# Rotary embedding on one core: the two leading fp32 positions on two hardware DMA queues, with one table on each

## The chip, the cores and the metric

The kernel runs on one core of a Trainium2 chip. The metric is the device time of one execution in microseconds (us). Before the change it was 317.61 us, the median of 3 runs (317.57 to 317.75).

The profile's span, from the first to the last instruction, is about 1.8 us shorter than the time of the same execution (316.0 us against 317.78 us in the profiled run of the kernel before). Spans are compared with spans below, and times with times.

## The reference

```python
# x: (8, 2048, 16, 64) fp32; cos, sin: (2048, 32) fp32
x1, x2 = x_pairs[..., 0], x_pairs[..., 1]        # neighbours in the last axis
out1 = x1 * cos - x2 * sin
out2 = x1 * sin + x2 * cos
out = np.stack([out1, out2], axis=-1)            # interleaved again, fp32
```

There is little arithmetic per byte. The input is 64 MiB and so is the output: 8 batches of 8 MiB each way.

## The kernel before

A partition holds 16 positions (K = 16) of 1024 values. Each batch is loaded by one transfer issued from GpSimd, which casts fp32 to bf16 on the way. VectorE rotates it in place with three bf16 instructions per four positions, and GpSimd issues the store, which casts back. Five batch tiles (NX = 5) are in use.

The first two positions of batch 0 go another way: as fp32 on the SP queue, then a cast on ScalarE (called ACT in the profile). The last four positions of the last batch leave as fp32 on the SP queue.

```python
    with tc.manual_schedule():
        head = stage.tile([P, TAIL, HD], fp32, name="st")
        for k in range(HEAD):                                   # HEAD = 2
            nc.sync.dma_start(out=head[:, k : k + 1], in_=x_t[0, :, k : k + 1])
        nc.sync.dma_start(out=cos_sb, in_=cos_t)
        nc.sync.dma_start(out=sin_sb, in_=sin_t)
        load(0, HEAD)                                           # GpSimd queue
        for b in range(1, NX):
            load(b)

        nc.scalar.copy(out=tiles[0][:, :HEAD], in_=head[:, :HEAD])
        # ... VectorE: s_tab from sin_sb (two instructions), c_tab from cos_sb ...
        for b in range(B):
            # ... rotate(b, ...) on VectorE, four positions at a time ...
            if b < B - 1:
                store(b)                                        # GpSimd queue
            if b >= 1 and b - 1 + NX < B:
                load(b - 1 + NX)                                # waits for store(b - 1)
        store(B - 1, K - TAIL)

        tail = stage.tile([P, TAIL, HD], fp32, name="st")
        nc.scalar.copy(out=tiles[B - 2][:1, 0, :1], in_=tiles[B - 1][:1, K - 1, :1])   # waits for store(B - 2)
        nc.scalar.copy(out=tail, in_=tiles[B - 1][:, K - TAIL :])
        nc.sync.dma_start(out=out_t[B - 1, :, K - TAIL :], in_=tail)
```

Of the kernel before, what the change touches and what calls it, by code (L numbers as in the profile page):

```python
# [2 lines left out]

# [4 lines left out]


@with_exitstack  # L10
def kernel(
    ctx: ExitStack,
    tc: tile.TileContext,
    x: bass.AP,
    cos: bass.AP,
    sin: bass.AP,
    out: bass.AP,
):
    nc = tc.nc
    fp32 = mybir.dt.float32  # L20
    bf16 = mybir.dt.bfloat16
    mult = mybir.AluOpType.mult
    add = mybir.AluOpType.add

    B, S, H, D = x.shape
    P = 128
    K = S // P
    KP = 4
    D2 = D // 2
    HD = H * D  # L30
    NX = 5
    HEAD = 2
    TAIL = 4


    x_t = x.rearrange("b (p k) h d -> b p k (h d)", p=P, k=K)
    out_t = out.rearrange("b (p k) h d -> b p k (h d)", p=P, k=K)
    cos_t = cos.rearrange("(p k) c -> p (k c)", p=P, k=K)
    sin_t = sin.rearrange("(p k) c -> p (k c)", p=P, k=K)

    consts = ctx.enter_context(tc.tile_pool(name="consts", bufs=1))
    xpool = ctx.enter_context(tc.tile_pool(name="xpool", bufs=NX))
    qpool = ctx.enter_context(tc.tile_pool(name="qpool", bufs=1))
    stage = ctx.enter_context(tc.tile_pool(name="stage", bufs=1))

    cos_sb = consts.tile([P, K * D2], fp32)
    sin_sb = consts.tile([P, K * D2], fp32)
    c_tab = consts.tile([P, K, D], bf16)
    s_tab = consts.tile([P, K, D], bf16)

    tiles = {}

    def load(b, k0=0):
        if b not in tiles:
            tiles[b] = xpool.tile([P, K, HD], bf16, name="xt")
        nc.gpsimd.dma_start(out=tiles[b][:, k0:], in_=x_t[b, :, k0:])  # L56

    def store(b, k1=K):
        nc.gpsimd.dma_start(out=out_t[b, :, :k1], in_=tiles[b][:, :k1])  # L59

    def rotate(b, k0, k1):
        nk = k1 - k0
        xp = tiles[b][:, k0:k1]
        qt = qpool.tile([P, KP, HD], bf16, name="qt")

        def rows(a):
            return a.rearrange("p k (h e) -> p k h e", h=H, e=D)

        def tab(a):
            return dataclasses.replace(  # L70
                a, offset=a.offset + k0 * D, ap=[a.ap[0], [D, nk], [0, H], [1, D]]
            )

        nc.vector.tensor_tensor(out=rows(qt[:, :nk]), in0=rows(xp), in1=tab(s_tab), op=mult)  # L74
        nc.vector.tensor_tensor(out=rows(xp), in0=rows(xp), in1=tab(c_tab), op=mult)  # L75
        q_swap = dataclasses.replace(
            qt, offset=qt.offset + 1, ap=[qt.ap[0], [2, nk * HD // 2], [-1, 2]]
        )
        x3 = xp.rearrange("p k (a j) -> p (k a) j", j=2)
        nc.vector.tensor_tensor(out=x3, in0=x3, in1=q_swap, op=add)  # L80

    with tc.manual_schedule():
        head = stage.tile([P, TAIL, HD], fp32, name="st")
        for k in range(HEAD):
            nc.sync.dma_start(out=head[:, k : k + 1], in_=x_t[0, :, k : k + 1])  # L85
        nc.sync.dma_start(out=cos_sb, in_=cos_t)
        nc.sync.dma_start(out=sin_sb, in_=sin_t)
        load(0, HEAD)
        for b in range(1, NX):
            load(b)  # L90

        nc.scalar.copy(out=tiles[0][:, :HEAD], in_=head[:, :HEAD])  # L92
        s2 = s_tab.rearrange("p k (i j) -> p (k i) j", j=2)
        nc.vector.tensor_copy(out=s2[:, :, 0], in_=sin_sb)  # L94
        nc.vector.tensor_scalar_mul(s2[:, :, 1], sin_sb, -1.0)  # L95
        nc.vector.tensor_copy(  # L96
            out=c_tab.rearrange("p k (i j) -> p (k i) j", j=2),
            in_=cos_sb.to_broadcast([P, K * D2, 2]),
        )
        for b in range(B):  # L100
            if b == 0:
                rotate(b, 0, HEAD)
                rotate(b, HEAD, KP)
            for k0 in range(KP if b == 0 else 0, K, KP):
                rotate(b, k0, k0 + KP)
            if b < B - 1:
                store(b)

            if b >= 1 and b - 1 + NX < B:
                load(b - 1 + NX)  # L110
        store(B - 1, K - TAIL)



        tail = stage.tile([P, TAIL, HD], fp32, name="st")
        nc.scalar.copy(out=tiles[B - 2][:1, 0, :1], in_=tiles[B - 1][:1, K - 1, :1])  # L116
        nc.scalar.copy(out=tail, in_=tiles[B - 1][:, K - TAIL :])  # L117
        nc.sync.dma_start(out=out_t[B - 1, :, K - TAIL :], in_=tail)


# [1 line left out]
_INS = ['x', 'cos', 'sin']  # L122
_OUTS = [((8, 2048, 16, 64), 'float32')]


# [23 lines left out]
```

## Time and profile before

| what | kernel before |
|---|---|
| measured time | 317.61 us |
| span of the profile | 316.0 us |
| VectorE busy | 70% |
| VectorE's wait for the sin table | 44.2 us |
| share of the DMA engines' span, GpSimd queue + hardware queue | 96.8% + 3.1% |
| HBM traffic | 67.63 MB read, 67.11 MB written |

The page of the kernel before begins so. Under "busy tenths", each column is a fortieth of the span:

```profile
DVE 221.8 (70%) x102; ACT 6.9 (2%) x4; POOL 8.9 (3%) x20
...
DVE  0000039999999999999999999999999999100000
...
DMA  9899999999999999999999999999999999999996
...
q0 software_dynamic: 2304, 98.04, 96.8%
q1 hardware_dynamic: 720, 3.67, 3.1%
...
HBM read 67.63 MB, written 67.11 MB: 426 GB/s over the span
```

Read the three kinds of line together. The DVE line (VectorE) has a visible hole at the start. The DMA line has none until the last slice. The queue lines say the same in numbers: 96.8% and 3.1% of 16 engines' span are 99.9%.

The view of waits names the hole:

```profile
ACT xt L116 <- DMA out_dram<-xt: 286.3, 1, 286.3
POOL out_dram L59 <- DVE xt L80: 202.1, 8, 70.5
POOL xt L56 <- DMA out_dram<-xt: 51.3, 3, 21.7
DVE s_tab L94 <- DMA sin_sb<-in_sin_dram: 44.2, 1, 44.2
...
```

Each line gives engine and line, what it waited for, us in total, number of waits, and the longest. VectorE waits once, for sin, and never for a batch load. The large waits of ACT and POOL (GpSimd) are waits of engines that have nothing else to do.

Three lines of the timeline: the issue of store 0, VectorE's last instruction, and the tail's cast (start, duration, engine and line, and in brackets the idle time before it and what ended it).

```profile
74.53 0.54 POOL L59 DMA_DIRECT2D out_dram<-xt  x1 [70.48 <-DVE xt L80]
...
267.11 2.29 DVE L80 TENSOR_TENSOR xt<-xt,qt 128x4096 bf16<-128x4096 bf16 x1
...
295.96 3.60 ACT L117 CAST st<-xt 128x4096 f32<-128x4096 bf16 x1
```

The DMA issues on the page say how long each transfer took from issue to landing (the last column, us):

```profile
xt<-in_x_dram POOLq DMA_DIRECT2D x1, 3584.0 KB, 22.7
...
st<-in_x_dram SPq DMA_DIRECT2D x2, 512.0 KB, 4.5
cos_sb<-in_cos_dram SPq DMA_DIRECT2D x1, 256.0 KB, 22.4
sin_sb<-in_sin_dram SPq DMA_DIRECT2D x1, 256.0 KB, 42.1
```

A table of 256 KB takes as long as a batch load of 3584 KB. The trace's DMA packet records explain it. They are summarised here by queue and size, from the kernel before:

```
queue    bytes written   packets   mean us   first start   last start
GpSimd   28672            128       2.130      5.14          21.43      (batch 0, 14 positions)
GpSimd   32768            896       2.437     22.78         235.04      (loads: 64 KB read, 32 KB written)
GpSimd   65536            896       2.447    101.24         292.96      (stores)
SP       2048             256       0.096      7.25          43.59      (the two tables, 8 packets each on every engine)
```

A table packet needs 0.096 us but is followed by a batch-load packet of over 2 us each time. The batch loads begin at 5.14 us, and the first table packet at 7.25 us, so every table packet pays that turn.

### The profile page before, as it was taken

What the parts mean: (1) busy time and instruction counts of PE and PEld (TensorE: products, weight loads), DVE (VectorE), ACT (ScalarE), POOL (GpSimd) and SP (SyncE); (2) the same over time, 40 slices, a digit from 0 to 9 for tenths busy, and PEclk for the clock granted to TensorE, in tenths of its full rate; (3) what the DMA queues carried; (4) which work ended last, traced back from release to release, by engine and by line L of the source; (5) the groups of instructions that cost most, each with busy time, mean ns of one, the idle gap of its engine ahead of it and who ended that gap; (6) DMA issues with size and microseconds to landing.
All of it is one profiled execution on the core that took longest, in us unless ns stands there. A gap on an engine that the chain in (4) does not pass through costs nothing.

```text
span 316.0 us, 198 instructions
## 1 busy us (share of the span) xinstructions
DVE 221.8 (70%) x102; ACT 6.9 (2%) x4; POOL 8.9 (3%) x20
## 2 busy tenths in 40 slices
DVE  0000039999999999999999999999999999100000
ACT  1200000000000000000000000000000000000400
POOL 3000000000000000000000000000000000000000
DMA  9899999999999999999999999999999999999996
GB/s 241 198 257 212 212 207 236 228 199 199 253 212 265 398 498 431 398 332 261 203 399 465 328 203 199 481 448 265 199 307 423 398 440 481 406 398 481 417 431 263
DMA packets 3025, 101.72 MB, mean 322 GB/s; under 512 B 336, under 2 KB 336, under 8 KB 848
## 3 DMA queue, kind: packets, MB, share of 16 engines
q0 software_dynamic: 2304, 98.04, 96.8%
q1 hardware_dynamic: 720, 3.67, 3.1%
q14 instruction: 1, 0.01, 0.0%
HBM read 67.63 MB, written 67.11 MB: 426 GB/s over the span
## 4 chain that ended last, share of the span: by engine, by line
another core or an unknown queue 91%; DMA 2%; ACTq 1%; ACT 1%; SPq 0%; issue 0%
DMA st<-in_x_dram 2%; ACTq L144 1%; ACT xt L92 1%; ACT L92 0%; SPq L85 0%; ACT xt L116 0%; ACTq L116 0%; ACTq L92 0%
## 5 line engine op out<-in xcount | busy, mean ns | idle before, releaser
L75 DVE TENSOR_TENSOR xt<-xt,c_tab 128x4096 bf16<-128x4096 bf16 (+1 forms) x33 | 73.5, 2228 | 1.1
L80 DVE TENSOR_TENSOR xt<-xt,qt 128x4096 bf16<-128x4096 bf16 (+1 forms) x33 | 73.5, 2228 | 1.1
L74 DVE TENSOR_TENSOR qt<-xt,s_tab 128x4096 bf16<-128x4096 bf16 (+1 forms) x33 | 73.5, 2228 | 1.1
L94 DVE CAST s_tab<-sin_sb 128x512 bf16<-128x512 f32 x1 | 0.5, 453 | 44.2 <-DMA sin_sb<-in_sin_dram 44.2
L59 POOL DMA_DIRECT2D out_dram<-xt x8 | 4.3, 535 | 202.1 <-DVE xt L80 202.1
L116 ACT COPY xt<-xt 1x1 bf16<-1x1 bf16 x1 | 0.2, 193 | 286.3 <-DMA out_dram<-xt 286.3
L56 POOL DMA_DIRECT2D xt<-in_x_dram x8 | 4.4, 561 | 52.1 <-DMA out_dram<-xt 51.3
L117 ACT CAST st<-xt 128x4096 f32<-128x4096 bf16 x1 | 3.6, 3599 | 0.0
L92 ACT CAST xt<-st 128x2048 bf16<-128x2048 f32 x1 | 1.9, 1899 | 0.0
L92 ACT ACT_TABLE_LOAD x1 | 1.3, 1283 | 6.4 <-DMA st<-in_x_dram 6.4
L96 DVE CAST c_tab<-cos_sb 128x1024 bf16<-128x1024 f32 x1 | 0.7, 684 | 0.0
L95 DVE TENSOR_SCALAR s_tab<-sin_sb 128x512 bf16<-128x512 f32 x1 | 0.4, 443 | 0.0
L133 POOL MEMSET const-float32-0.0<- 128x1 f32 x1 | 0.1, 99 | 0.2 <-issue 0.2
L133 POOL MEMSET const-bfloat16-1.0<- 128x1 bf16 x1 | 0.1, 102 | 0.0
L133 POOL MEMSET const-float32-1.0<- 128x1 f32 x1 | 0.1, 99 | 0.0
L133 POOL MEMSET const-uint8-127<- 128x1 uint8 x1 | 0.1, 99 | 0.0
## 6 DMA issues: line engine op xcount, KB each, us to landing
xt<-in_x_dram POOLq DMA_DIRECT2D x7, 4096.0 KB, 58.0
out_dram<-xt POOLq DMA_DIRECT2D x1, 6144.0 KB, 49.4
xt<-in_x_dram POOLq DMA_DIRECT2D x1, 3584.0 KB, 22.7
out_dram<-st SPq DMA_DIRECT2D x1, 2048.0 KB, 15.5
st<-in_x_dram SPq DMA_DIRECT2D x2, 512.0 KB, 4.5
cos_sb<-in_cos_dram SPq DMA_DIRECT2D x1, 256.0 KB, 22.4
sin_sb<-in_sin_dram SPq DMA_DIRECT2D x1, 256.0 KB, 42.1
out_dram<-xt POOLq DMA_DIRECT2D x7, 54.0
```

The lines of the kernel that those rows point to most:

```text
L56: nc.gpsimd.dma_start(out=tiles[b][:, k0:], in_=x_t[b, :, k0:])
L59: nc.gpsimd.dma_start(out=out_t[b, :, :k1], in_=tiles[b][:, :k1])
L74: nc.vector.tensor_tensor(out=rows(qt[:, :nk]), in0=rows(xp), in1=tab(s_tab), op=mult)
L75: nc.vector.tensor_tensor(out=rows(xp), in0=rows(xp), in1=tab(c_tab), op=mult)
L80: nc.vector.tensor_tensor(out=x3, in0=x3, in1=q_swap, op=add)
L92: nc.scalar.copy(out=tiles[0][:, :HEAD], in_=head[:, :HEAD])
L94: nc.vector.tensor_copy(out=s2[:, :, 0], in_=sin_sb)
L95: nc.vector.tensor_scalar_mul(s2[:, :, 1], sin_sb, -1.0)
L96: nc.vector.tensor_copy(out=c_tab.rearrange("p k (i j) -> p (k i) j", j=2), in_=cos_sb.to_broadcast([P, K * D2, 2]),)
L117: nc.scalar.copy(out=tail, in_=tiles[B - 1][:, K - TAIL :])
L133: nc = _bacc.Bacc("TRN2", target_bir_lowering=False, num_devices=1)
L144: with _tile.TileContext(nc) as tc:
```

## The change

The intent is to bring the head (the two fp32 positions) and the tables in sooner by using both hardware queues: each carries one head position and then one table.

```diff
         for k in range(HEAD):
-            nc.sync.dma_start(out=head[:, k : k + 1], in_=x_t[0, :, k : k + 1])
+            q = (nc.sync, nc.scalar)[k % 2]
+            q.dma_start(out=head[:, k : k + 1], in_=x_t[0, :, k : k + 1])
         nc.sync.dma_start(out=cos_sb, in_=cos_t)
-        nc.sync.dma_start(out=sin_sb, in_=sin_t)
+        nc.scalar.dma_start(out=sin_sb, in_=sin_t)
```

## The prediction

> **What bounds the kernel now.** The DMA engines, from end to end. The page's queue table gives the GpSimd queue 96.8% and the hardware queue 3.1% of the 16 engines' span. HBM traffic is 67.63 + 67.11 MB: 426 GB/s over 316 us. The trace's packet records show why this does not move: a batch load reads 64 KB per packet in 2.437 us and a store writes 64 KB in 2.447 us, so 16 engines do about 430 GB/s either way. The GpSimd queue's packets run from 5.14 to 311.76 us; per engine their durations add to about 305.3 us, so that queue is never empty. VectorE is busy 70% and idle for 44.2 us at the start, a wait for the sin table (view of waits). That is the most visible hole, but not what the span waits for.
>
> **Why the tables are late.** Each table is 8 packets of 2 KB per engine, 0.096 us each, and each takes its turn with a 64 KB-read packet of the batch loads: 8 x (2.437 + 0.096) = 20.3 us per table. On one queue cos lands at 24.1 us and sin at 44.2 us. The Trainium skill (DMA: Bandwidth & Descriptors, "Queues, rings and completion order") says an engine goes round its queues packet by packet; this trace agrees, 20.1 us between the landings.
>
> **What the change does.** No byte, packet or compute instruction is added. One head position and sin go from the SP to the Activation queue (two issues of about 0.4 us each move). The tables now take turns beside each other, so both land at about 24 us. VectorE starts at 24-25 us instead of 44.2 and runs 20 us ahead. Batch 0's remaining load landed at 23.9 us, so it is no obstacle.
>
> **How much is on the critical path.** Nearly nothing. The GpSimd queue is served in order: loads 0-4 until 102 us, then store 0, store 1, load 5, store 2, load 6 and so on. Store 0 will be issued at about 54 instead of 74.5 us but still starts at 102. Load 5 waits for store 0 to land (121.5 us) as before. The 20 us come back as VectorE waits: load 6 landed at 199.1 us, VectorE would want it at 194 (about 5 us); load 7 landed at 237.8 against 227 (about 11 us). VectorE ends at about 266 instead of 269.4 us. Store 6 still lands at about 296 us; the tail's cast (3.6 us) waits for that, then comes the 15.5 us tail store. The skill (same page, "Issuing engines are not separate DMA queues") says that another issuing engine saves only issue time.
>
> What can move is the first 5 us, before the GpSimd queue starts: table packets may pass before 5.14 us. Estimate: all 16 per engine would save 16 x 0.096 = 1.5 us, a few 0.2-0.4 us.
>
> **Predicted:** 317.3 us, 8 in 10 within 316.3 to 318.1. Faster by over 2%: 2%; within 2%: 97%; slower: 1%.
>
> **What would show it.** Right: VectorE's wait for a table falls from 44.2 to about 24 us; cos and sin both land about 22 us after issue; new VectorE waits on batch loads of about 16 us in all near 194-238 us; the GpSimd queue's share stays near 97%; the tail's cast still starts near 296 us. Wrong: sin still at 44 us, or VectorE without new waits.
>
> **What would make it wrong.** GpSimd-queue packets other than 2.44 us with three queues active; a start of that queue other than 5.1 us; descriptor writing on GpSimd slowed by VectorE being busy from 24 us; a fixed cost of a second hardware queue.

## The result, and the profile after

The changed kernel takes 317.64 us (median of 6 runs, 317.57 to 317.95) against 317.60 us for the kernel before (median of 6, 317.56 to 317.75). The ratio is 1.0002, 95% interval 0.9989 to 1.0015: the same.

The page after:

```profile
DVE 221.8 (70%) x102; ACT 6.9 (2%) x4; POOL 8.8 (3%) x20
...
DVE  0009999999999999999999994799708996000000
...
DMA  9999999999999999999999999999999999999997
...
q0 software_dynamic: 2304, 98.04, 97.0%
q1 hardware_dynamic: 432, 2.88, 2.4%
q10 hardware_dynamic: 288, 0.79, 0.6%
...
HBM read 67.63 MB, written 67.11 MB: 427 GB/s over the span
```

The hole in the DVE line is half as long at the start, and new holes have opened about two thirds of the way through. The DMA line is as full as it was. The new queue q10 is the Activation queue.

The waits after:

```profile
ACT xt L117 <- DMA out_dram<-xt: 286.8, 1, 286.8
POOL out_dram L59 <- DVE xt L80: 153.9, 5, 50.0
POOL xt L56 <- DMA out_dram<-xt: 95.6, 3, 39.7
DVE s_tab L95 <- DMA sin_sb<-in_sin_dram: 23.8, 1, 23.8
DVE qt L74 <- DMA xt<-in_x_dram: 16.7, 2, 10.8
```

VectorE's wait for sin fell by 20.4 us (44.2 to 23.8). Two waits for batch loads, 16.7 us together, are new. The rest of the 20.4 us is idle time after its last instruction: VectorE began its last add at 263.26 us instead of 267.11, 3.85 us sooner. 16.7 + 3.85 is 20.5 us. GpSimd shows the same thing from the other side: it waits 48.2 us less for VectorE (202.1 to 153.9) and 44.3 us more for stores to land (51.3 to 95.6).

In the timeline after, the two new waits look like this:

```profile
23.77 0.45 DVE L95 CAST s_tab<-sin_sb 128x512 bf16<-128x512 f32 x1 [23.77 <-DMA sin_sb<-in_sin_dram]
...
54.07 0.54 POOL L59 DMA_DIRECT2D out_dram<-xt  x1 [50.03 <-DVE xt L80]
...
199.03 2.29 DVE L74 TENSOR_TENSOR qt<-xt,s_tab 128x4096 bf16<-128x4096 bf16 x1 [5.92 <-DMA xt<-in_x_dram]
...
237.67 2.29 DVE L74 TENSOR_TENSOR qt<-xt,s_tab 128x4096 bf16<-128x4096 bf16 x1 [10.76 <-DMA xt<-in_x_dram]
...
263.26 2.29 DVE L80 TENSOR_TENSOR xt<-xt,qt 128x4096 bf16<-128x4096 bf16 x1
...
295.78 3.60 ACT L118 CAST st<-xt 128x4096 f32<-128x4096 bf16 x1
```

Store 0 is issued at 54.07 us instead of 74.53. It joins a queue that still has 48 us of loads in it. The tail's cast starts at 295.78 us (295.96 before).

The landings of the GpSimd queue's transfers, read from the trace, show where nothing moved (us from the start of the span):

```
          load 1   load 3   load 4   store 0   load 5   load 6   load 7   store 6
before    44.03    82.62   102.18    121.51   160.89   199.13   237.78   295.77
after     43.31    81.96   102.35    121.70   160.29   198.93   237.57   295.58
```

Loads 1 to 3 land 0.7 us sooner, because more packets of the hardware queues now pass before the batch loads start. Behind that start there were 256 table packets and 27 head packets before, 1.80 us of packet time per engine; after, there are 203 and 1, 1.16 us. By load 4 that lead is gone. Experiments e10 and e11 look at this.

### The profile page after: what moved, and what is told of

Its sections match the earlier page's. It is cut to its first block, busy times and chain, and to the rows that moved or that the text cites. A ratio compares the mean times of both kernels' runs of the same rounds, so it can differ in the third digit from the quotient of the medians.

```text
span 315.8 us, 198 instructions
## 1 busy us (share of the span) xinstructions
DVE 221.8 (70%) x102; ACT 6.9 (2%) x4; POOL 8.8 (3%) x20
## 4 chain that ended last, share of the span: by engine, by line
another core or an unknown queue 91%; DMA 2%; ACTq 1%; ACT 1%; issue 0%
DMA st<-in_x_dram 2%; ACTq L145 1%; ACT xt L93 1%; ACT L93 0%; ACT xt L117 0%; ACTq L117 0%; ACTq L93 0%
## 5 line engine op out<-in xcount | busy, mean ns | idle before, releaser
L74 DVE TENSOR_TENSOR qt<-xt,s_tab 128x4096 bf16<-128x4096 bf16 (+1 forms) x33 | 73.5, 2228 | 17.7 <-DMA xt<-in_x_dram 16.7
L95 DVE CAST s_tab<-sin_sb 128x512 bf16<-128x512 f32 x1 | 0.5, 454 | 23.8 <-DMA sin_sb<-in_sin_dram 23.8
L59 POOL DMA_DIRECT2D out_dram<-xt x8 | 4.3, 533 | 153.9 <-DVE xt L80 153.9
L56 POOL DMA_DIRECT2D xt<-in_x_dram x8 | 4.4, 560 | 96.4 <-DMA out_dram<-xt 95.6
```

The lines of the kernel that those rows point to most:

```text
L56: nc.gpsimd.dma_start(out=tiles[b][:, k0:], in_=x_t[b, :, k0:])
L59: nc.gpsimd.dma_start(out=out_t[b, :, :k1], in_=tiles[b][:, :k1])
L74: nc.vector.tensor_tensor(out=rows(qt[:, :nk]), in0=rows(xp), in1=tab(s_tab), op=mult)
L95: nc.vector.tensor_copy(out=s2[:, :, 0], in_=sin_sb)
```

## The experiments

The theory ("DMA-bound"): the GpSimd queue never runs dry, so the time is the start of that queue plus its bytes plus the tail, and VectorE has slack. The rivals: (a) VectorE's chain does set the span; (b) the earlier VectorE start is worth something, and a third queue costs as much again, so that the two cancel.

### e1 and e2: each part of the change alone

e1, against the kernel before:

```diff
-        nc.sync.dma_start(out=sin_sb, in_=sin_t)
+        nc.scalar.dma_start(out=sin_sb, in_=sin_t)
```

> Part alone: only the sin table moves to the Activation queue, both head positions stay on SP. DMA-bound theory: sin gets a turn of its own, so it and cos take their turns beside each other and VectorE's wait for a table ends near 24 us, as in the full change; time 317.3 to 317.9 us all the same. Rival 'the earlier VectorE start does save time and a third queue eats it': also a third queue, so no difference in time, but load packets longer than 2.437 us. Rival 'VectorE-bound': faster than before by several us.

e2, against the changed kernel:

```diff
-        nc.scalar.dma_start(out=sin_sb, in_=sin_t)
+        nc.sync.dma_start(out=sin_sb, in_=sin_t)
```

> Part alone: only the second head position moves to the Activation queue, both tables stay on SP one behind the other. DMA-bound theory: cos lands near 20 us as after (some of its packets pass before the batch loads start), sin follows it and lands near 40 us; VectorE starts near 40 us; time 317.3 to 317.9 us. So the 20 us of VectorE start come from the sin move, and neither part moves the time.

Measured: e1 317.49 us, ratio to before 1.0001 (0.9986 to 1.0016). e2 317.78 us, ratio 1.0011 (0.9994 to 1.0027). Both times are as expected. The VectorE waits of e1 were not as I expected:

```profile
DVE c_tab L96 <- DMA cos_sb<-in_cos_dram: 25.2, 1, 25.2
...
DVE qt L74 <- DMA xt<-in_x_dram: 9.2, 1, 9.2
DVE s_tab L94 <- DMA sin_sb<-in_sin_dram: 5.8, 1, 5.8
```

In e1 sin has its queue to itself and lands at 5.8 us, ahead of the batch loads. Cos lands at 31.8 us, not 24, because the second head position is in front of it on the SP queue and took until 13.2 us. In e2 sin landed at 35.7 us (expected near 40).

So my attribution in e2's text, that all 20 us come from the sin move, was wrong. VectorE has its last table 12.4 us sooner through the sin move alone (44.2 to 31.8) and 8.5 us sooner through the head move alone (44.2 to 35.7). Together the change gives 20.4. Each part takes packets off the SP queue, and it is the number of packets in front that counts. Neither part moves the time. The load packets of e1 last 2.437 us as before, but that is no test of rival (b): sin's last packet ended at 5.3 us and the first batch-load packet started at 5.6, so the Activation queue was empty by then. The changed kernel is the better witness. There both hardware queues take turns with batch 0's load, whose packets last 2.138 us in the mean, 2.130 before. That is under 0.1 us per engine over its 8 packets.

### e3: the tables ahead of the head

```diff
         head = stage.tile([P, TAIL, HD], fp32, name="st")
+        nc.sync.dma_start(out=cos_sb, in_=cos_t)
+        nc.scalar.dma_start(out=sin_sb, in_=sin_t)
         for k in range(HEAD):
             ...
-        nc.sync.dma_start(out=cos_sb, in_=cos_t)
-        nc.scalar.dma_start(out=sin_sb, in_=sin_t)
```

> The full change with the tables issued ahead of the head positions. DMA-bound theory: all table packets pass before the GpSimd queue starts near 5.1 us, so the tables land before 5 us and VectorE's wait for a table is under 5 us (then it waits for the head's cast near 10 us and for batch 0's load near 24 us); at most 1 us gained: 316.6 to 317.9 us. Rival 'an early VectorE start saves time': clearly below the change, by several us.

Measured: 317.58 us, ratio 1.0003 (0.9988 to 1.0018). The tables landed as expected, at 4.1 and 4.2 us. The head paid for it: its positions landed at 13.4 and 17.8 us, which I had not expected (I had the cast near 10 us). Their packets now take turns with the batch loads. An even earlier VectorE start than the change's is worth nothing: store 0 is issued at 49.5 us and still waits for its place.

### e4: the same cos bytes in twice as many packets

```diff
-        nc.sync.dma_start(out=cos_sb, in_=cos_t)
+        half = K * D2 // 2
+        for i in range(2):
+            nc.sync.dma_start(out=cos_sb[:, i * half : (i + 1) * half], in_=cos_t[:, i * half : (i + 1) * half])
```

> The full change, with cos sent as two transfers of half the columns, so 16 packets of 1 KB per engine in place of 8 of 2 KB, the same bytes. If the queues take turns by packet, cos needs twice the turns that come after the batch loads start, and lands near 40 us (19.75 us in the change), sin stays near 24 us. If they share by bytes, cos stays near 20 us. Time 317.3 to 318.0 us either way by the DMA-bound theory.

Measured: 317.61 us (one look). Sin landed at 23.6 us, cos at 33.3 us. The view of waits has the extra 9 us:

```profile
DVE s_tab L97 <- DMA sin_sb<-in_sin_dram: 23.6, 1, 23.6
DVE c_tab L99 <- DMA cos_sb<-in_cos_dram: 9.0, 1, 9.0
```

The bytes are the same and the packets half as long (0.053 us), and cos came 13.5 us later than the change's 19.75. (In e7, e8 and e10, which issue the same transfers of head and tables as the change, cos landed at 17.4 to 17.6 us, so its landing varies by about one turn; 33.3 is far outside that.) That is less than the "near 40" of my expectation, since more of the small packets passed before the batch loads started, but it is clear of "stays near 20". The queues take turns by packet, not by bytes.

### e5, e6, e7: an added load on VectorE

e5 and e6 add dummy multiplies to the kernel before (n = 5 and 14), e7 adds the 14 to the changed kernel. They run after the tables are built, on a part of the head tile that is not used. Results stay right.

```diff
             in_=cos_sb.to_broadcast([P, K * D2, 2]),
         )
+        nc.vector.memset(head[:, HEAD:], 0.0)
+        for _ in range(n):
+            nc.vector.tensor_tensor(out=head[:, HEAD:], in0=head[:, HEAD:], in1=head[:, HEAD:], op=mult)
```

> The kernel before with five dummy VectorE multiplies on an unused part of the head tile after the tables, about 11 us of VectorE (estimate: 2.2 us each, as 128x4096 bf16 took 2.29). Results stay right. DMA-bound theory: store 1 was issued at 102.2 us and its turn comes near 121 us, so VectorE has about 17 us of slack; time 317.3 to 318.0 us. Rival 'VectorE's chain sets the span': plus 11 us, near 329 us.

> The same with fourteen, about 31 us of VectorE. DMA-bound theory: stores 0 and 1 are issued near 105.5 and 133 us, after the GpSimd queue has run dry near 102 and again near 127 us; the queue stands idle for 133 - 121[...]: plus 13 to 17 us, 330 to 335 us. VectorE-bound rival: plus 31 us, 348 us. Contention rival: no prediction but plus 31 us as well if VectorE was on the path.

> The changed kernel with the same fourteen dummy multiplies. DMA-bound theory: VectorE starts 20 us sooner, so its slack is about 37 us and the same burden costs nothing: 317.3 to 318.5 us, with the new waits on loads 6 and 7 gone. Against the kernel before with the same burden the change then gains 13 to 17 us. If the change's 20 us were really lost to contention, this kernel would be about as slow as the other burdened one.

| run | delay of store 0's issue | time | ratio to before |
|---|---|---|---|
| e5, before + 5 | 88.23 - 74.53 = 13.7 us | 317.54 us | one look |
| e6, before + 14 | 109.06 - 74.53 = 34.5 us | 334.82 us | 1.0541 (1.0526 to 1.0557) |
| e7, after + 14 | 89.05 - 54.07 = 35.0 us | 317.68 us | 1.0007 (0.9992 to 1.0022) |

Store 0's issue in e5, e6 and e7, in this order:

```profile
88.23 0.54 POOL L59 DMA_DIRECT2D out_dram<-xt  x1 [84.20 <-DVE xt L80]
...
109.06 0.54 POOL L59 DMA_DIRECT2D out_dram<-xt  x1 [105.02 <-DVE xt L80]
...
89.05 0.54 POOL L59 DMA_DIRECT2D out_dram<-xt  x1 [85.02 <-DVE xt L80]
```

This is the deciding set. The kernel before absorbs 13.7 us of VectorE delay for nothing. Of 34.5 us it passes on 17.25 us (334.82 - 317.57), so its slack is about 17.3 us. The changed kernel absorbs 35.0 us, and its waits for loads 6 and 7 are gone, as expected.

The queue can be seen running dry in e6. The windows (columns: window, its length, busy us of VectorE, ACT and POOL, clock, DMA share, GB/s), first e6:

```profile
96.00:100.00 4.00, 3.93 (x3) 0.00 (x0) 0.00 (x0) 1.00 1.03 221
102.00:108.00 6.00, 5.93 (x3) 0.00 (x0) 0.00 (x0) 1.00 0.00 0
110.00:128.00 18.00, 17.73 (x9) 0.00 (x0) 0.00 (x0) 1.00 1.09 466
131.00:136.00 5.00, 4.93 (x3) 0.00 (x0) 0.00 (x0) 1.00 0.00 0
```

and e7:

```profile
...
102.00:108.00 6.00, 5.90 (x4) 0.00 (x0) 0.00 (x0) 1.00 0.82 350
...
131.00:136.00 5.00, 4.93 (x3) 0.00 (x0) 0.00 (x0) 1.00 0.98 419
...
```

In e6 the DMA share is 0.00 in two windows where VectorE is busy throughout. By the packet records the two dry spells last from 101.48 to 110.17 us and from 129.63 to 137.81 us. That is 16.9 us together, which is the 17.25 us of added time but for 0.4. In e7 the same two windows are busy. So the earlier VectorE start does have a value (17.1 us between e6 and e7), but only as slack that this kernel does not use. Rival (a) would have had 348 us for e6 by the estimate made before the run, and 352 by the measured delay. Rival (b), with a cost as large as the 17 us, would have left e7 about as slow as e6. Both fall. A cost of a few tenths is not excluded by this; e10 and e11 come to it.

The runs also speak to one of the prediction's doubts, that descriptor writing on GpSimd suffers while VectorE is busy. In e6 the first packets of stores 0 and 1 started 1.1 us after their issue (109.06 to 110.17, 136.71 to 137.81) while VectorE was busy, which is sooner than the 3.9 us at the start of the kernel, where it was idle.

### e8: half a store less

```diff
-                store(b)
+                store(b, K // 2 if b == 3 else K)
```

> The changed kernel with half of batch 3's store left out (4 MB; the result is wrong on purpose). DMA-bound theory: 8 packets per engine become half as long, 8 x 1.22 us = 9.8 us less: 307.4 to 308.4 us, although no VectorE or load instruction changes. VectorE-bound rival or a bound set by the arrival of loads 6 and 7 alone: 317.6 us, or less only so far as load 7 comes sooner.

Measured: 307.85 us, ratio 0.9692 (0.9676 to 0.9708). The result is wrong. The 9.72 us saved are the 9.8 us that the packets' lengths gave. No load and no compute instruction was taken away. Bytes in the GpSimd queue count one for one. By itself e8 does not tell the queue from a bound set by load 7's arrival and the VectorE work behind it: load 7 landed at 227.96 us (237.57 in the change) and VectorE's last instruction started at 253.64 us, both 9.6 us sooner. e5 and e7 do tell them apart: their last VectorE instruction started at 280.81 and 281.63 us, 13.7 and 18.4 us later than without the added load, and the time stayed.

### e9: the first GpSimd transfer cut in two

```diff
-        load(0, HEAD)
+        nc_first = 4
+        tiles[0] = xpool.tile([P, K, HD], bf16, name="xt")
+        nc.gpsimd.dma_start(out=tiles[0][:, HEAD:nc_first], in_=x_t[0, :, HEAD:nc_first])
+        load(0, nc_first)
```

> Try for a better version: batch 0's load on the GpSimd queue is cut in two, positions 2-3 first. If the 4 us from issue to that queue's first packet grow with the size of the first transfer, the queue starts sooner, by up to 1 us, and the time falls to 316.6 to 317.4 us. If they are fixed, nothing is gained and the smaller packets cost a little: 317.5 to 318.2 us.

Measured: 317.56 us, ratio 1.0007 (0.9995 to 1.0020). The queue's first packet started at 5.30 us (5.23 in the change), so the 4 us from issue to first packet did not shrink with the size of the first transfer. The tables landed at 8.4 and 9.6 us here, since the first turns are short, and that again bought nothing.

### e10 and e11: where the 0.7 us of lead go

The packet records show the place. The last packet of load 4 on each engine normally takes 2.43 us. With store 0 queued behind it, it takes 2.51 to 3.05 us in the kernel before and 3.12 to 3.52 us in the changed one. Summed over the packets in that window the excess per engine is 0.32 us before and 0.92 us after. The difference, 0.60 us, is the lead, give or take 0.1 us (0.65 us by packet time, 0.7 by the landings). In e6, where no store stands behind load 4, these packets take 2.43 us.

e10, against the changed kernel, reads 1 MB less ahead of store 0:

```diff
+            if b == 2:
+                tiles[b] = xpool.tile([P, K, HD], bf16, name="xt")
+                nc.vector.memset(tiles[b][:, K - 2 :], 0.0)
+                nc.gpsimd.dma_start(out=tiles[b][:, : K - 2], in_=x_t[b, :, : K - 2])
+            else:
+                load(b)
```

> In the change, load 1 lands 0.7 us sooner than before, and at store 0 that lead is gone: the last packets of load 4 took up to 3.5 us in place of 2.43. Here the changed kernel reads two positions less of batch 2 (1 MB; zeros from VectorE in their place, the result is wrong on purpose), 8 packets per engine shorter by an eighth, 8 x 0.30 = 2.4 us. If every us saved ahead of store 0 counts, store 0's first packet starts near 98.9 us and the time is 315.0 to 315.5 us. Rival 'store 0 cannot start before about 101 us, so whatever is saved ahead of it is lost': 317.3 to 317.9 us, with load 4's last packets stretched by 3 us.

e11, against the changed kernel, puts store 0 ahead of load 4:

```diff
-        for b in range(1, NX):
+        for b in range(1, NX - 1):
             load(b)
 ...
                 store(b)
+            if b == 0:
+                load(NX - 1)
```

> The changed kernel with load 4 issued after store 0 (VectorE now has batch 0 ready at 54 us, before loads 0 to 3 end at 82). The same bytes in another order, so the DMA-bound theory says 317.2 to 318.0 us. If the stretch of the last load packets belongs to the first passage from loads to stores, it shows near 82 us, in load 3's last packets; if it belongs to five loads in a row or to a time near 101 us, it is gone or stays near 101 us.

Measured: e10 315.18 us, ratio 0.9927 (0.9915 to 0.9939), result wrong. That is 2.3 us less than the kernel before in the same rounds (317.47), where the shorter packets gave 2.4. Store 0's first packet started at 98.98 us (101.31 in the change), and load 4's last packets took 3.15 to 3.69 us. So what is saved ahead of store 0 does count, and the rival of a fixed start near 101 us falls. e11 317.39 us, ratio 0.9997 (0.9984 to 1.0011). The stretch moved along: it stands in load 3's last packets (up to 3.66 us, excess 0.87 us per engine), with store 0's first packet at 81.77 us, and load 4's packets are normal.

The stretch thus belongs to the first passage from loads to stores. Later passages (load 5 to store 2 near 160 us, load 7 to store 4 near 238 us) have no excess above 0.02 us. What causes it, no run here settles. Its excess was 0.24 to 0.32 us per engine in the three runs with both head positions on the SP queue and a store waiting behind load 4 (before, e1, e5), and 0.59 to 1.14 us in all runs with one position on the Activation queue. That is an observation; its reason stays open too. It means that a cost of some 0.6 us which comes with the head's move, and takes back the lead, is not ruled out. The difference is 0.2% of the time.

None of the variants with a right result beats both kernels by anything clear of the noise.

## Why the prediction was right

- **The bound.** Right. The time follows the GpSimd queue's bytes (e8: 9.72 us for 9.8) and its dry spells (e6: 17.25 us for 16.9).
- **Turns by packet.** Right in kind: e4 shows that turns go by packet, not by byte. Predicted landings were about 24 us for both tables, measured 23.74 us for sin and 19.75 us for cos. The four us on cos are packets that passed before the batch loads started: 53 of the 256 table packets (47 of cos, 6 of sin) started before the first GpSimd packet, none in the kernel before. That sin came so close to 24 is partly luck. Its turns lasted 2.2 to 2.3 us, since batch 0's packets are the shorter ones (2.14 us), and not the 2.53 us of the prediction's sum. But the 4-byte record that closes the transfer on each engine took one more turn, which the sum does not have (last data packet at 21.2 us, last closing record at 23.4).
- **Where the 20 us go.** Right: waits of 5.9 and 10.8 us for loads 6 and 7 (predicted 5 and 11), and an end of VectorE 3.85 us sooner (predicted about 3.4).
- **Slack.** The prediction did not give it as one figure. It gave that store 0 would still start at 102 us, and store 0's first packet came at 101.3.
- **The first five us.** This term was mis-sized, within the range. The prediction's 317.3 us counted on a net gain of a few tenths from table packets. The lead ahead of store 0 is in fact larger, 0.7 us: the table packets gave 0.39 us of packet time per engine, at the top of the estimate, and head packets, which the prediction did not count, 0.26 us. But 0.6 us is lost again at the first passage from loads to stores, which it did not foresee. These two misses nearly cancel, and that part of the agreement is luck. The measured difference of 0.04 us is not clear of noise. Nor is the 0.2 us between the two profiles' spans (316.0 and 315.8) a rest of the lead: at store 0's landing the changed kernel was 0.2 us behind.
- **A cost of the third queue.** None is visible in the time. Load packets are 2.448 us in the mean after and 2.437 before. Nearly all of that difference lies in those last packets of load 4, and whether the head's move causes it is open.

The Trainium skill (DMA: Bandwidth & Descriptors, "Issuing engines are not separate DMA queues") was a good guide to the time, and incomplete for the landing of a small transfer. The last section comes back to it.

## What to carry to other kernels

The largest wait of a compute engine is not the bound while the DMA queue behind it never runs dry: look for the resource with no hole in it, and ask whether the change takes anything off that. Work that starts sooner behind an in-order queue only waits there, and turns up as new waits on the next loads. A second queue does bring a small transfer in sooner beside large ones, since turns go by packet, so it is worth having where that transfer does gate the DMA stream (here only under added load: 334.82 us in e6, 317.68 in e7).

## What the Trainium skill lacked or had wrong

- DMA: Bandwidth & Descriptors, "Issuing engines are not separate DMA queues" says that starting DMAs from several engines will "only save the time on the sequencer it takes to initiate the DMA". That held for the total time (ratio 1.0002). It leaves out latency: with the head and the tables on two queues, each with its own turns, sin landed at 23.7 us instead of 44.2.
- The same page, "SWDGE vs HWDGE vs iDMA" gives a packet as 4096 B or less by preference. In this trace the records of batch loads, which set the turns, are 32768 B written (65536 B read) and 2.44 us long, so a 2 KB table packet of 0.096 us waits up to 25 times its length at each turn. The page says that turns go by packet; it does not say that they can be so unequal.
- The same page, "Specifications" has a first-byte latency of about 1 us for the GpSimd path. Here the queue's first transfer of the kernel had 3.9 us from issue to first packet (1.24 to 5.14 us), and cutting it smaller did not help (e9: 5.30 us). A later store onto an empty queue had 1.1 us (e6: 109.06 to 110.17 us). The page does not tell a first transfer from later ones.
- The same page, "Where 436 GB/s comes from" says that for transfers between HBM and SBUF the limit of about 358 GB/s binds. That figure is half of a stack's 716 GB/s, and the note under the page's own measurements gives it as each core's share with both cores streaming. It did not bind here: this kernel moves 427 GB/s of HBM traffic over its whole span on one core, in line with the 425 GB/s that the page measured on a single core.
- No page has the stretch of the last load packets at the first passage from loads to stores: 2.43 us normally, up to 3.75 us there (e2).
